# The last pairs of two squared-ReLU layers and the step to the recurrence: another order of the products, sums and transpositions

## The chip, the cores and the metric

The kernel runs on one core of a Trainium2 chip. The time is what the device needs for one execution, in microseconds (us); before the change it is 1073.29 us, the median of three runs (1073.25 to 1073.98). The engines of the core are TensorE (PE, matmuls, with its weight loads listed as PEld), VectorE (DVE), ScalarE (ACT), GpSimd (POOL) and SyncE (SP, which here only issues loads and stores). Each works through its own list of instructions in order and waits for the others through semaphores.

## The reference

A trunk of two layers over 512 tokens of width 1024, float32 throughout:

```
h = x
for layer in (0, 1):
    hn = rmsnorm(h, norm_mix[layer])
    mix = chunked_band_attention(hn, ...) if layer == 0 else rglru_block(hn, ...)
    h = h + mix
    h = h + sq_relu_mlp(rmsnorm(h, norm_mlp[layer]), w1, w2)
return rmsnorm(h, norm_final)

sq_relu_mlp(h, w1, w2):  z = relu(h @ w1);  return (z * z) @ w2      # 1024 -> 4096 -> 1024
```

The recurrent block of layer 1 projects to 2 x 1024 columns, sends one half through a causal convolution, gates and a scan, the other through a gelu, multiplies them and projects back. The change touches the two MLPs and the passage from the MLP of layer 0 to the recurrence.

## The kernel before

**Numbers.** A float32 operand is split into a high part (a rounding copy on ScalarE) and a low part (a subtraction on VectorE), and each product is three matmuls: high x high, high x low, low x high (`mm3`, line 214). So every weight passes through one ScalarE instruction (line 140, tile `wh`) and one VectorE instruction (line 143, tile `wl`).

**Weights.** They stand in one list, `plan`, in the order of use. `want(n)` (line 152) takes the next n entries and first issues the split of those ahead of them, `state["ahead"]` entries far (5 in an MLP, and in the recurrence after it). The tiles `wh` and `wl` come from a ring of five, and in an MLP from two more; a split has to wait until the matmuls on an older entry of its ring place are through. Plain entries are loaded by SP into three raw tiles (`wr`) and split there.

**The MLP** (`mlp`, line 601). The hidden width is worked through in four pairs p of two blocks of 512. An up tile `up(p, j)` (line 632) is 24 matmuls, then relu and square on ScalarE into the tile `a`. Tiles 0 to 3 of a pair make the first block, 4 to 7 the second. The down product of the pair is a 2 x 2 block product done with seven block products in place of eight: of the activation blocks 11, 12, 22 and the combinations s1 to s4, and of the weight blocks 11, 21, 22 and the combinations t1 to t4. Combinations of weights are made in place on the raw blocks (line 138), those of activations on VectorE (lines 679, 680, 682), and each activation operand is split again (`split`, line 658: tiles `h`, `h0`, `h1`, `h2` and `l`, `nn`, `g`, `f`, `c`).

`round_(p)` (line 649) does one pair: the tiles `up(p, 4)` to `up(p, 7)`, and after every second one the combinations of the chunk that is ready; then seven products through `step(name, bank, ...)`, in the order 11, 12, s1, s4, s2, s3, 22, each 24 matmuls into PSUM banks X, Z or Y. After each, `read` (line 627) adds the banks to the running result `d` in token order. A bank that goes on accumulating (X and Y) may only be written again when it has been read. In pairs 0 to 2 the up tiles 0 to 3 of the next pair are put between the later products; in the last pair there are none left, and there each product is done for one tile of 128 tokens after the other (`ts=(t,)`), with a read after each.

After the last pair of layer 0, `turns` (line 741) brings the result back to the transposed residual (`back`, 32 transpositions on TensorE, adds at line 755), and already does the norm's splits (`n1.split`), the first half of four projections of the recurrence (`open_x`, line 827: banks `xb0` to `xb3`, over tiles 4 to 7) and the squares for the norm (`n1.square`). After the last pair of layer 1, `ends` (line 776) does the final norm and the stores.

**The recurrence** (line 919 on) finishes the projections `xb0` to `xb3` with 12 matmuls each. After number 2 comes `n1.sums` (line 266: eight small matmuls that sum the squares per token, a root, a reciprocal), after number 3 `n1.rstd` (line 275: eight matmuls that spread it into a row, and a copy); then the convolutions start, whose first instruction (`xp`, line 866) reads a bank `xb` and multiplies it with the row. Later projections reuse those banks.

**The order.** The program is written as one sequence, but a scheduler works out each engine's list from it: what stands earlier goes first, and where it isn't ready by the scheduler's own reckoning, something later that is ready takes the place. Buffers are given out at the first write.

Of the kernel before, what the change touches and what calls it, by code (L numbers as in the profile page):

```python
# [18 lines left out]
KT = D // P  # L19
# [21 lines left out]
def trunk(ctx: ExitStack, tc: tile.TileContext, xT, cols, gfin, win, wqkv, wo, rwin, rga, rgx, rwo, w1, w2, out):  # L41
# [55 lines left out]
    plan = []  # L97
# [81 lines left out]
    def add_mlp(layer):  # L179
        starts.append(len(plan))  # L180
        def up_(p, j):
            c0 = 2 * p * T + j * P
            plan.append(("plain", KT, [w1[layer][:, c0 : c0 + P]]))

        for j in range(4):
            up_(0, j)
        for p in range(4):
            for j in range(4, 8):
                up_(p, j)
            srcs = [  # L190
                w2[layer][(2 * p + k) * T : (2 * p + k + 1) * T, c * T : (c + 1) * T]
                for k, c in ((0, 0), (1, 0), (0, 1), (1, 1))
            ]
            for n, kind in enumerate(("11", "21", "t1", "22", "t2", "t3", "t4")):
                for half in range(2):
                    plan.append((kind, half, srcs))
                if p < 3 and 2 <= n <= 5:
                    up_(p + 1, n - 2)
# [87 lines left out]
    with ExitStack() as actx:  # L286
# [199 lines left out]
        for k0, nk in FIRST:  # L486
            WH, WL = want(1)
# [113 lines left out]
    def mlp(ly, norm):  # L601
        with ExitStack() as mctx:
# [46 lines left out]
            def round_(p):  # L649
                A, low, raw = {}, {}, {}  # L650

                def room(n, kind, tag):
                    return (wk if tag == "nn" else zp).tile([P, 4, U], kind, name=f"{tag}{n}{ly}{p}", tag=tag)

                def place(n, h, l):
                    low[n] = (room(n, F32R, h), room(n, F32R, l))

                def split(n, ks=slice(0, 4)):
                    H, L = low[n]
                    S.copy(H[:, ks], raw[n][:, ks])  # L660
                    V.tensor_sub(L[:, ks], raw[n][:, ks], f(H[:, ks]))

                first, second = a[p, 0], None
                raw["11"], raw["s1"] = first[:, 0], first[:, 1]
                for n, tag in (("s3", "c"), ("s2", "f"), ("s4", "g")):
                    raw[n] = room(n, F32, tag)
                ins = V.tensor_sub(raw["s3"], raw["11"], raw["s1"])
                if (ly, p) == (0, 1):
                    constants(ins)
                place("11", "h0", "l")  # L670
                split("11")
                place("12", "h1", "nn")
                for j in range(4, 8):
                    up(p, j)
                    raw["12"], raw["22"] = a[p, 1][:, 0], a[p, 1][:, 1]
                    if j % 2:
                        ks = slice(j - 5, j - 3)
                        r = {n: raw[n][:, ks] for n in raw}
                        V.tensor_sub(r["s2"], r["22"], r["s3"])
                        V.tensor_sub(r["s4"], r["12"], r["s2"])  # L680
                        split("12", ks)
                        V.tensor_add(r["s1"], r["s1"], r["22"])
                Y, X = ([atp(f"{b}{ly}{p}{t}") for t in range(2)] for b in "yx")
                Z = [mmp(f"z{ly}{p}{t}") for t in range(2)]
                held = {}

                def product(name, bank, fresh, ts=(0, 1)):
                    if not held.get(name):
                        held[name] = [want(1) for part in range(2)]
                    H, L = low[name]  # L690
                    for part in range(2):
                        WH, WL = held[name][part]
                        for k in range(2):
                            for t in ts:
                                c = slice(t * P, (t + 1) * P)
                                kk_ = 2 * part + k
                                mm3(bank[t], H[:, kk_, c], L[:, kk_, c], WH(k, slice(0, T)), WL(k, slice(0, T)),
                                    fresh and kk_ == 0, kk_ == 3, True)

                def ahead(j):  # L700
                    if p < 3:
                        up(p + 1, j)


                def step(name, bank, fresh, t0, c):
                    if p < 3:
                        product(name, bank, fresh)
                    for t in range(2):
                        if p == 3:
                            product(name, bank, fresh, ts=(t,))  # L710
                        read(bank[t], t0 + t, c)


                step("11", X, True, 0, 0)
                place("s1", "h0", "l")
                split("s1")
                step("12", Z, True, 0, 0)
                place("s4", "h1", "nn")
                split("s4")
                step("s1", Y, True, 2, 1)  # L720
                place("s2", "h2", "g")
                split("s2")
                place("s3", "h0", "f")
                split("s3")
                ahead(0)
                step("s4", Y, False, 0, 1)
                place("22", "h1", "c")
                split("22")
                ahead(1)
                step("s2", X, False, 0, 1)  # L730
                ahead(2)
                if p == 3:

                    (ends if ly else turns)(step, product, X)
                    return
                step("s3", X, False, 2, 1)
                ahead(3)
                step("22", X, False, 2, 0)


            def turns(step, product, X):
                banks = [atp(f"back{i}") for i in range(2)]
                n = [0]

                def back(qs, h):
                    for q in qs:
                        x = banks[n[0] % 2]
                        n[0] += 1
                        for i in range(2):
                            c, cs = columns(2 * q + i)  # L750
                            for t in range(2):
                                j = 2 * i + t
                                PE.transpose(x[:, j * P : (j + 1) * P], dt[2 * h + t, c][:, cs], ident)
                        hv = hT2[q][:, :, h * U : (h + 1) * U]
                        V.tensor_add(hv, x.rearrange("p (i c) -> p i c", i=2), hv)

                step("s3", X, False, 2, 1)
                back(range(4), 0)
                product("22", X, False, ts=(0,))
                read(X[0], 2, 0)  # L760
                back((2, 3), 1)
                tc.keep_in_program_order(S.activation(spare, epsb, AF.Sqrt))
                product("22", X, False, ts=(1,))
                read(X[1], 3, 0)
                for m in range(4, KT):
                    n1.split(m)
                open_x(0)
                back((0, 1), 1)
                for m in range(4):
                    n1.split(m)  # L770
                open_x(1)
                for m in range(KT):
                    n1.square(m)


# [40 lines left out]
            for p in range(4):  # L816
# [1 line left out]
                    gfins = per.tile([P, 4, T], F32, name="gfins", tag="hx0")  # L818
                    nc.sync.dma_start(gfins[:, 0:2], gfin.rearrange("p (c n) -> p c n", c=2))
                round_(p)  # L820
            state.update(more=None)

    n1 = Norm("n1", C_MIX1)
    xbs = []
# [1 line left out]

    def open_x(u):
        WH, WL = want(1)
        accs = [mmp(f"xb{2 * u + i}") for i in range(2)]
        project(accs, PAIR, WH, WL, [(hnH[k], hnL[k]) for k in range(4, KT)], last=False)  # L830
        xbs.extend(accs)

    mlp(0, nm1)

# [2 lines left out]
    with ExitStack() as rctx:  # L837
# [83 lines left out]
        for u in range(4):  # L921
            WH, WL = want(2 if u > 1 else 1)
            for i in range(2):
                c = 2 * u + i
                if i == 1 and u < 3:
                    gate_weights(u + 1)
                acc = xbs[c] if c < 4 else (atp if c == 4 else mmp)(f"xb{c}")
                project([acc], PAIR[i : i + 1], WH, WL, xs if c > 3 else xs[:4], first=c > 3)
                if c < 2:
                    continue  # L930
                if c == 2:
                    n1.sums()
                if c == 3:
                    rr.append(n1.rstd())
                    for j in range(4):
                        cv[j] = conv(j, xbs[j])
                        if j >= 2:
                            gate(j - 2, *cv[j - 2])
                if c >= 4:
                    gate(c - 2, *cv[c - 2])  # L940
                    cv[c] = conv(c, acc)
                if c == 5:
                    decay(range(4))
# [81 lines left out]
```

## Time and profile before

| what | value |
|---|---|
| median of three runs | 1073.29 us |
| the profiled execution's own time | 1074.18 us |
| its span in the trace | 1072.4 us |
| busy: TensorE, VectorE, ScalarE | 1056.1, 799.9, 587.2 us |
| mean granted TensorE clock | 0.993 |
| TensorE's waits of more than 1 us after the start | 3.08, 1.88 and 2.83 us |
| TensorE's last matmul to the end of the span | 6.8 us |

The span is the time from the first to the last instruction of one execution that the profiler followed. A row of the trace gives the start and the duration of an instruction in us, engine, source line, operation, output and inputs by the names of the program's tiles, and in square brackets how long its engine had been idle before it and what ended that. Matmuls overlap: each shows some 0.39 us, but they start 0.23 us apart. The granted clock is the share of its full rate that TensorE got.

### The profile page before, as it was taken

The page shows a single profiled execution, that of the slowest core. Times are in us where ns is not written, and L with a number is a line of the kernel's source. Part 1 is how long each engine was busy: PE and PEld are TensorE (multiplying, and loading weights), DVE is VectorE, ACT ScalarE, POOL GpSimd, SP SyncE. Part 2 cuts the span into 40 slices and gives each one's busy share as a digit, 9 for nine tenths or more (in the row PEclk, how much of TensorE's full clock was granted, in tenths as well). Part 3 has the DMA queues.
Part 4 walks back from the last instruction along what each step waited for, and adds up shares of the span by engine and source line. Part 5 has one row for each costly group of instructions (what it writes and reads, how often), then busy time and mean ns, then how long its engine had stood idle before and what let it go on. Part 6 is the DMA issues. An engine that isn't in the chain of part 4 may idle for free.

```text
span 1072.4 us, 12842 instructions
## 1 busy us (share of the span) xinstructions
PE 1056.1 (98%) x4820; PEld 875.6 (82%) x4820; DVE 799.9 (75%) x1168; ACT 587.2 (55%) x886; POOL 9.0 (1%) x28
## 2 busy tenths in 40 slices
PE   9999999999999999999999999999999999999996
PEld 8888888888888888888877788888888888888884
DVE  6899779866595695596498799984396497487486
ACT  6667567555554554454454598555463454454454
POOL 0010000000000000000000000000000000000000
PEclk9999999999999999999999999999999999999998
DMA  8344253264044045045003313283136036025002
GB/s 276 99 138 132 65 177 99 79 208 126 20 154 141 7 132 177 1 127 187 1 1 117 99 60 98 79 270 87 37 98 200 17 92 202 20 81 174 1 1 79
DMA packets 128413, 111.51 MB, mean 104 GB/s; under 512 B 4320, under 2 KB 104672, under 8 KB 128352
## 3 DMA queue, kind: packets, MB, share of 16 engines
q1 hardware_dynamic: 127776, 109.99, 33.4%
q8 instruction: 38, 0.62, 0.2%
q10 hardware_dynamic: 576, 0.72, 0.2%
q14 instruction: 23, 0.19, 0.1%
HBM read 104.39 MB, written 2.10 MB: 99 GB/s over the span
## 4 chain that ended last, share of the span: by engine, by line
PE 92%; DVE 6%; ACT 1%; issue 1%; DMA 0%; POOL 0%; ACTq 0%; POOLq 0%
PE u L215 11%; PE u L216 11%; PE u L217 11%; PE x L215 5%; PE x L217 5%; PE x L216 5%; PE y L215 2%; PE y L216 2%; PE y L217 2%; PE x L437 2%; PE xb L215 1%; PE xb L217 1%; PE xb L216 1%; PE wo L215 1%; PE wo L216 1%; PE ro L215 1%
## 5 line engine op out<-in xcount | busy, mean ns | idle before, releaser
L140 ACT CAST wh<-b 128x1024 fp32r<-128x1024 f32 x112 | 117.6, 1051 | 184.9 <-PE u L216 137.0
L143 DVE TENSOR_TENSOR wl<-wr,wh 128x1024 fp32r<-128x1024 f32 (+1 forms) x122 | 146.6, 1205 | 89.8 <-ACT wh L140 78.1
L143 DVE TENSOR_TENSOR wl<-b,wh 128x1024 fp32r<-128x1024 f32 x112 | 136.6, 1222 | 102.4 <-ACT wh L140 102.4
L140 ACT CAST wh<-wr 128x1024 fp32r<-128x1024 f32 (+1 forms) x121 | 125.4, 1038 | 141.8 <-PE u L216 58.2
L215 PE MATMUL u<-hnH,wh 128*128 128x512 f32 x512 | 200.3, 391 | 0.0
L217 PE MATMUL u<-hnH,wl 128*128 128x512 f32 x512 | 199.6, 390 | 0.0
L216 PE MATMUL u<-hnL,wh 128*128 128x512 f32 x512 | 199.4, 390 | 0.0
L217 PEld LDWEIGHTS u<-hnH,wl 128*128 128x128 f32 x512 | 96.1, 188 | 20.3
L215 PEld LDWEIGHTS u<-hnH,wh 128*128 128x128 f32 x512 | 96.1, 188 | 19.7
L216 PEld LDWEIGHTS u<-hnL,wh 128*128 128x128 f32 x512 | 96.2, 188 | 19.6
L138 DVE TENSOR_TENSOR b<-b,b 128x1024 f32<-128x1024 f32 x64 | 76.7, 1223 | 1.3 <-DMA b<-in_w 1.3
L215 PE MATMUL x<-wh,h 128*128 128x512 f32 x128 | 50.1, 391 | 0.0
L216 PE MATMUL x<-wl,h 128*128 128x512 f32 x128 | 50.0, 390 | 0.0
L627 DVE SCALAR_TENSOR_TENSOR d<-x,rq,d 128x512 f32<-128x512 f32 x60 | 42.8, 745 | 3.5 <-PE x L217 3.5
L639 ACT ACTIVATE a<-u 128x512 f32<-128x512 f32 x64 | 37.8, 590 | 13.3 <-PE u L217 13.3
L640 ACT ACTIVATE a<-a 128x512 f32<-128x512 f32 x64 | 40.6, 635 | 1.8
L417 ACT ACTIVATE p<-p,mx 128x128 f32<-128x128 f32 (+1 forms) x64 | 35.2, 552 | 6.2 <-DVE mx L414 6.0
L215 PE MATMUL x<-wh,h0s 128*128 128x512 f32 x64 | 26.5, 414 | 5.9 <-DVE d L627 5.9
L660 ACT CAST h<-a 128x1024 fp32r<-128x1024 f32 (+1 forms) x32 | 26.8, 836 | 6.5 <-PE y L216 5.7
L410 DVE CUSTOM_DVE_ANT_0 p<-s,bias 128x128 f32<-128x128 f32 (+1 forms) x64 | 27.7, 485 | 3.2 <-PE s L407 2.9
L441 ACT CAST pH<-x 128x512 fp32r<-128x512 f32 (+1 forms) x48 | 21.7, 517 | 13.5 <-PE x L437 13.4
L215 PEld LDWEIGHTS x<-wh,h 128*128 128x128 f32 x128 | 24.0, 188 | 4.9
(342 smaller groups left out, 2301.4 us busy)
## 6 DMA issues: line engine op xcount, KB each, us to landing
wr<-in_w SPq DMA_DIRECT2D x64, 512.0 KB, 4.0
b<-in_w SPq DMA_DIRECT2D x64, 512.0 KB, 4.2
wr<-in_wqkv SPq DMA_DIRECT2D x20, 512.0 KB, 3.8
wr<-in_rwin SPq DMA_DIRECT2D x16, 512.0 KB, 3.4
wr<-in_wo SPq DMA_DIRECT2D x8, 512.0 KB, 4.1
wr<-in_rwo SPq DMA_DIRECT2D x8, 512.0 KB, 3.5
x<-in_xT SPq DMA_DIRECT2D x8, 256.0 KB, 3.9
bias<-in_win SPq DMA_DIRECT2D x4, 512.0 KB, 4.7
```

The lines of the kernel that those rows point to most:

```text
L138: V.tensor_sub(raw, raws[x, half], raws[y, half])
L140: S.copy(H[:, :n], raw[:, :n])
L143: low = V.tensor_sub(L[:, :n], raw[:, :n], f(H[:, :n]))
L215: PE.matmul(acc, WH, XH, start=start, stop=False, skip_group_check=more)
L216: PE.matmul(acc, WH, XL, start=False, stop=False, skip_group_check=more)
L217: PE.matmul(acc, WL, XH, start=False, stop=stop, skip_group_check=more)
L410: V.tensor_tensor_reduce(out=pt[:, seg[t] : seg[t] + n], in0=sc[t], in1=b[:, h % 4, T - n :], scale=1.0, scalar=-3.0e38, op0=ALU.add, op1= ...
L417: S.activation(pt[:, seg[t] : seg[t] + n], pt[:, seg[t] : seg[t] + n], AF.Exp, bias=mx[:, t : t + 1], accum_out=sm[:, t : t + 1],)
L627: V.scalar_tensor_tensor(d, acc, r, d, ALU.mult, ALU.add)
L639: S.activation(c, acc.rearrange("p (h c) -> p h c", h=2), AF.Relu)
L640: S.activation(c, c, AF.Square)
L660: S.copy(H[:, ks], raw[n][:, ks])
```

## The change

Six edits:

1. In the list of weights the two halves of "11" of the last pair stand between the up tiles 5 and 6 in place of behind 7. With them go the eight loads of that pair's blocks, which are issued with the first half of "11".
2. The up tiles 4 to 7 are now written behind the definition of `step`, and "11" is done inside their loop: behind tile 7 in pairs 0 to 2 (as before), behind tile 5 in the last pair.
3. In the last pair the activation combinations of the second half are made in two quarters, after tiles 6 and 7, in place of one half after tile 7.
4. In the last pair "12" is done for both token tiles together; the other products there stay one tile after the other.
5. The lookahead in the list of weights goes from 5 to 3 ahead of "s1" of the last pair, and is 4 in the recurrence (5 before).
6. In `turns`, the projections `xb0` and `xb1` are opened one after the other with the last transpositions between them; the squares of tiles 4 to 7 come ahead of `xb2`, those of 0 to 3 behind `xb3`. In the recurrence the sums come after projection 1 (before: 2) and the row after 2 (before: 3).

```diff
         for p in range(4):
-            for j in range(4, 8):
-                up_(p, j)
             srcs = [
...
+            for j in range(4, 8):
+                up_(p, j)
+                if j == (5 if p == 3 else 7):
+                    plan.extend(("11", half, srcs) for half in range(2))
-            for n, kind in enumerate(("11", "21", "t1", "22", "t2", "t3", "t4")):
+            for n, kind in enumerate(("21", "t1", "22", "t2", "t3", "t4"), 1):
...
                 place("12", "h1", "nn")
-                for j in range(4, 8):
-                    up(p, j)
-                    raw["12"], raw["22"] = a[p, 1][:, 0], a[p, 1][:, 1]
-                    if j % 2:
-                        ks = slice(j - 5, j - 3)
...
                 def step(name, bank, fresh, t0, c):
-                    if p < 3:
+                    apart = p == 3 and name != "12"
+                    if not apart:
                         product(name, bank, fresh)
                     for t in range(2):
-                        if p == 3:
+                        if apart:
                             product(name, bank, fresh, ts=(t,))
                         read(bank[t], t0 + t, c)
-                step("11", X, True, 0, 0)
+                chunks = {5: slice(0, 2), 7: slice(2, 4)} if p < 3 else {5: slice(0, 2), 6: slice(2, 3), 7: slice(3, 4)}
+                for j in range(4, 8):
+                    up(p, j)
+                    raw["12"], raw["22"] = a[p, 1][:, 0], a[p, 1][:, 1]
+                    if j in chunks:
+                        ks = chunks[j]
+                        r = {n: raw[n][:, ks] for n in raw}
+                        V.tensor_sub(r["s2"], r["22"], r["s3"])
+                        V.tensor_sub(r["s4"], r["12"], r["s2"])
+                        split("12", ks)
+                        V.tensor_add(r["s1"], r["s1"], r["22"])
+                    if j == (5 if p == 3 else 7):
+                        step("11", X, True, 0, 0)
...
                 split("s4")
+                if p == 3:
+                    state["ahead"] = 3
                 step("s1", Y, True, 2, 1)
...
-                open_x(0)
+                opening = open_x(0)
+                next(opening)
                 back((0, 1), 1)
                 for m in range(4):
                     n1.split(m)
-                open_x(1)
-                for m in range(KT):
+                next(opening)
+                for m in range(4, KT):
+                    n1.square(m)
+                for _ in open_x(1):
+                    pass
+                for m in range(4):
                     n1.square(m)
...
-            state.update(more=None)
+            state.update(more=None, ahead=4)
...
     def open_x(u):
         WH, WL = want(1)
-        accs = [mmp(f"xb{2 * u + i}") for i in range(2)]
-        project(accs, PAIR, WH, WL, [(hnH[k], hnL[k]) for k in range(4, KT)], last=False)
-        xbs.extend(accs)
+        for i in range(2):
+            xbs.append(mmp(f"xb{2 * u + i}"))
+            project(xbs[-1:], PAIR[i : i + 1], WH, WL, [(hnH[k], hnL[k]) for k in range(4, KT)], last=False)
+            yield
...
-                if c < 2:
-                    continue
-                if c == 2:
+                if c == 1:
                     n1.sums()
-                if c == 3:
+                if c == 2:
                     rr.append(n1.rstd())
+                if c == 3:
                     for j in range(4):
```

More of the change, by code (lines that the diff above doesn't have):

```diff
@@ L672, in round_ @@
                 place("12", "h1", "nn")
-                for j in range(4, 8):
-                    up(p, j)
-                    raw["12"], raw["22"] = a[p, 1][:, 0], a[p, 1][:, 1]
-                    if j % 2:
-                        ks = slice(j - 5, j - 3)
[L678 to L682, printed above, removed]
                 Y, X = ([atp(f"{b}{ly}{p}{t}") for t in range(2)] for b in "yx")
@@ L928, in trunk @@
                 project([acc], PAIR[i : i + 1], WH, WL, xs if c > 3 else xs[:4], first=c > 3)
-                if c < 2:
-                    continue
+                if c == 1:
+                    n1.sums()
                 if c == 2:
-                    n1.sums()
+                    rr.append(n1.rstd())
                 if c == 3:
-                    rr.append(n1.rstd())
                     for j in range(4):
```

## The prediction

> **What bounds the kernel now.** I read the page first, then the list of what TensorE waited for, then the time slices around those waits, and last the order of VectorE's work in them.
>
> ```profile
> span 1072.4 us, 12842 instructions
> ...
> PE 1056.1 (98%) x4820; PEld 875.6 (82%) x4820; DVE 799.9 (75%) x1168; ACT 587.2 (55%) x886; POOL 9.0 (1%) x28
> ```
>
> TensorE is busy for 98% of the span and the change takes no matmul away, so only its idle time and its slow time can be won.
>
> ```profile
> PE x L215 <- DVE d L627: 5.9, 2, 3.1
> PE xb L215 <- DVE xp L866: 1.9, 1, 1.9
> ...
> 565.41 0.47 PE L215 MATMUL x<-wh,h0s 128*128 128x512 f32 x1 [3.08 <-DVE d L627]
> 606.44 0.50 PE L215 MATMUL xb<-hnH,wh 128*128 128x512 f32 x1 [1.88 <-DVE xp L866]
> 1052.75 0.47 PE L215 MATMUL x<-wh,h0s 128*128 128x512 f32 x1 [2.83 <-DVE d L627]
> ```
>
> There are three gaps worth the name. Two are one place in the two MLPs: in the last pair, product "s3" (weights `h0s`) goes into the same banks X that "s2" filled, and must wait until VectorE has read "s2" out (line 627). The third is in the recurrence, where the next projection waits for a PSUM bank that the first convolution input (line 866) frees.
>
> ```profile
> core 0: us, PE busy (x) PEld busy (x) DVE busy (x) ACT busy (x) POOL busy (x), PEclk, DMA share, GB/s
> 534.00:561.40 27.40, 27.40 (x122) 22.50 (x121) 26.30 (x29) 16.06 (x17) 0.00 (x0) 1.00 0.00 1
> 565.40:579.80 14.40, 14.38 (x64) 11.88 (x65) 12.71 (x16) 5.04 (x7) 0.00 (x0) 0.88 0.53 165
> 606.40:620.00 13.60, 13.56 (x52) 11.00 (x53) 12.69 (x23) 9.14 (x13) 0.00 (x0) 0.87 0.12 40
> ...
> 1000.90:1022.80 21.90, 21.90 (x98) 18.14 (x97) 9.77 (x12) 8.58 (x12) 0.00 (x0) 1.00 0.00 1
> 1022.80:1049.90 27.10, 27.10 (x120) 21.96 (x118) 26.33 (x29) 14.44 (x17) 0.00 (x0) 1.00 0.00 0
> 1052.80:1065.60 12.80, 12.73 (x48) 9.99 (x48) 8.91 (x19) 6.99 (x19) 0.00 (x0) 0.87 0.22 83
> ```
>
> Two things stand here. Behind each gap the granted clock is 0.87 or 0.88, not 1.00: 0.12 x 14.4, 0.13 x 13.6 and 0.13 x 12.8 are each about 1.7 us more. And during the five products before the gap (1022.8 to 1049.9) VectorE is busy for 26.33 of 27.1 us, while in the four up tiles before (1000.9 to 1022.8) it is busy for 9.77 of 21.9. It isn't short of time in the round as a whole; it has its idle time too early. One product or up tile is 24 matmuls: 24 x 27.1 / 120 = 5.42 us.
>
> What the three gaps cost: (3.08 + 1.7) + (1.88 + 1.7) + (2.83 + 1.7) = 12.9 us. That is all that this change can win.
>
> **"11" between up tiles 5 and 6** (last pair, both layers). The prices of VectorE's work in the crowded stretch of layer 1, from 1020 to 1053:
>
> ```profile
> L143 DVE TENSOR_TENSOR wl<-b,wh 128x1024 fp32r<-128x1024 f32 x7 | 8.4, 1220 | 4.2 <-ACT wh L140 4.2
> L138 DVE TENSOR_TENSOR b<-b,b 128x1024 f32<-128x1024 f32 x6 | 7.2, 1220 | 0.0
> L627 DVE SCALAR_TENSOR_TENSOR d<-x,rq,d 128x512 f32<-128x512 f32 x4 | 2.9, 748 | 0.0
> ```
>
> Start to start a 128x1024 subtraction takes 1.13 us, a read-out 0.66, a 128x512 one 0.62 (from the rows of the chain below, 1026.54 to 1028.93). From 1023.51 to the end of the read-out at 1052.6 VectorE never stops: 29.1 us. What of it falls before the end of the last up tile once "11" has moved: two read-outs of X (1.3), half of the last pair of differences (four 128x512 operations become eight, of which four 128x256 stay behind: 2.5 less 1.5 is 1.0), and the weight work that TensorE's releases allow. A weight cast waits for a free buffer, that is for the matmuls seven weights back (the row at 1022.43 below); with "11" two up tiles earlier, the two weights that now wait for the last up tile and for "11" get their buffers 4 to 5 us earlier, so their low parts (2.3) and the block difference behind the first (1.1) go ahead too. The lookahead of 3 instead of 5 puts the last block difference (1.1) behind the read-out. 29.1 - 6.8 = 22.3 us remain, and start about 1 us after the last up tile, at 1028.9 in old times: they end at 1051.2, and TensorE wants the bank at 1049.9 (1052.75 - 2.83). That alone would leave 1.3 us of the gap.
>
> The other four block differences (4.5 us) decide. They need only raw blocks that are there and already split, so they can run while VectorE idles, as two already do now:
>
> ```profile
> 484.00:490.00 6.00, 3.60 (x3) 1.00 0.91 286
> 490.00:539.00 49.00, 0.00 (x0) 1.00 0.20 62
> 539.00:563.00 24.00, 6.76 (x6) 1.00 0.00 1
> ```
>
> (Slices of line 138 alone in layer 0: stretch, VectorE busy, count.) Each pair has eight such differences; only six of the last pair's stand after 539, so two of the three at 484 to 490 are its own, run 35 us before the weights made of them. In the new order VectorE has, between 1019 and 1029 in old times, 10 us less one low part, one block difference and 1.5 us of activation differences, some 6 us, for these four. Two of them are enough. I take the gap as gone in both layers: -4.8 and -4.5. If none goes early, 1.3 of it stays.
>
> **What now waits.** "11" was the cover between the last up tile and what is made of it. Before, "11" and "12" (10.8 us) lay ahead of "s1"; now "12" alone, 5.42.
>
> ```profile
> 1022.43 1.05 ACT L140 CAST wh<-b 128x1024 fp32r<-128x1024 f32 x1 [3.23 <-PE u L216]
> 1023.39 0.59 ACT L639 ACTIVATE a<-u 128x512 f32<-128x512 f32 x1
> 1024.01 0.63 ACT L640 ACTIVATE a<-a 128x512 f32<-128x512 f32 x1
> 1027.87 1.05 ACT L660 CAST h0s<-a 128x1024 fp32r<-128x1024 f32 x1
> ...
> 1024.68 0.69 DVE L679 TENSOR_TENSOR fs<-a,cs 128x512 f32<-128x512 f32 x1
> 1026.54 0.69 DVE L682 TENSOR_TENSOR a<-a,a 128x512 f32<-128x512 f32 x1
> 1028.93 0.75 DVE L627 SCALAR_TENSOR_TENSOR d<-x,rq,d 128x512 f32<-128x512 f32 x1
> 1029.60 1.22 DVE L661 TENSOR_TENSOR ls<-a,h0s 128x1024 fp32r<-128x1024 f32 x1
> ```
>
> From the end of the up tile (1022.8) to the first difference 1.9 us; four small ones some 1.5 (between 1.2 and 2.5: half the row, or the row); the cast `h0s` 1.0; the low part `ls` 1.2: 5.6 us. "s1" needs `ls` with its third matmul, 5.42 + 0.45 = 5.9 us after the up tile. So it just fits with nothing in between; each weight cast or subtraction in front costs about 1 us. Bounds: 0, and 2.0 (two in front) with 1.7 of slow clock behind it, 3.7 a layer. I take one in front, 0.9 a layer, because both engines' queues hold such work and take it when it is ready: +1.8. Behind the waiting matmul stand all of TensorE's, so it counts in full. "12" itself needs its last quarter only after 18 of its 24 matmuls (4.1 us), and that is made after 1.9 + 1.2: hidden, and that it runs over both token tiles together is what gives these 4.1 us; one by one it would be 2.0.
>
> The eight block loads of that pair now stand ahead of two weight loads in SP's queue:
>
> ```profile
> b<-in_w SPq DMA_DIRECT2D x64, 512.0 KB, 4.2
> ```
>
> These two weights are wanted some 30 us later, against 4.2 us a load: nothing. For the first three pairs the order is the same as before: nothing.
>
> **The step to the recurrence.**
>
> ```profile
> 599.84 0.95 PE L259 MATMUL n1ss<-ones,n1acc 128*128 128x2 f32 x8
> 604.60 0.59 ACT L280 COPY n1acc<-n1row 128x512 f32<-128x512 f32 x1
> ...
> 585.95 0.69 DVE L755 TENSOR_TENSOR h<-back,h 128x512 f32<-128x512 f32 x1 [3.19 <-PE back L753]
> 595.64 3.08 DVE L246 TENSOR_TENSOR n1acc<-n1acc,n1sq 128x512 f32<-128x512 f32 x4
> 604.56 1.23 DVE L143 TENSOR_TENSOR wl<-wr,wh 128x1024 fp32r<-128x1024 f32 x1 [3.26 <-PE n1row L278]
> 605.71 1.28 DVE L866 TENSOR_TENSOR xp<-xb,n1acc 128x512 f32<-128x512 f32 x2
> ```
>
> Sums and row each move ahead of one half projection (12 matmuls, 2.71 us). After the row comes that projection; the row's copy (0.59) and `xp` (0.66) need 1.3 to 1.5 us with the waits between, and the low part that now stands in front of `xp` is released only by the projection behind. So 1.2 us of slack, and the gap goes: -3.6. The sums, now wanted 2.71 us earlier, at 597.1, need the squares' last addition (598.7 now) 1.6 us earlier: four squares are put before the last transpositions' results, where VectorE idles 3.19 us, room for three additions of 0.6. It fits by little. Opening the projections one after the other halves the time in which the normalised tiles 4 to 7 are needed: between 0 and 1.2 us (two tiles late by a read-out); +0.3, as one is made every 0.66 us (a VectorE pass of 128x512) and used every 0.68 (three matmuls). The recurrence keeps one weight less ahead: from 0 to 1.2, +0.2, since TensorE shows no wait there.
>
> **The sum.** -12.9 + 1.8 + 0.3 + 0.2 = -10.6. The profiled execution took 1074.18 us (span 1072.4 and 1.8 around it), so 1063.6; the median of the three runs, 1073.29, lies 0.9 below it, so **1062.7**.
>
> **The rivals.**
> - *The four differences do not run early.* The order on VectorE is the scheduler's, and its stretch stays full. Then 1.3 us of each gap stays, without the slow clock or with it: 1062.7 + 2 x (1.3 to 3.0) = 1065.3 to 1068.7, say 1067. For it: 26.33 of 27.1 busy; against: the two that ran 35 us early. 0.17.
> - *The row isn't earlier in effect.* If the additions end at 598.7 as now, TensorE waits 1.6 us at the sums: 1062.7 + 3.6 = 1066.3. For it: ACT's and VectorE's other work (weights, gate weights) stands among the squares; against: the 3.19 us idle. 0.11.
> - *The slow clock after the two shorter gaps has another cause* and stays: 1062.7 + 2 x 1.7 = 1066.1. Against it: 0.87 stands right behind each of them, and 1.00 ahead. 0.03. [...]
> - *The wait moves to the head of "s1" and is longer there: slower.* What runs early may stand in front of the short chain: if six block differences come between the last up tile and `ls`, 6 x 1.13 - 0.3 = 6.5 us of wait and 1.7 of slow clock in each layer, 16.4 against 12.9 won: 1073.3 + 3.5 = 1077. It decides from 4.7 us of wait a layer on, four to five pieces in front. Against it: the chain comes first in the program, and differences are ready earlier. 0.08.
> - *Nothing changes.* If the scheduler already takes what is ready, the new program order may come out as the old one: 1073.3. Against it: the up tiles and "11" run in written order now. 0.08.
>
> **How the numbers follow.** The forecast has 0.53; its own range is 1060.4 (no new wait) to 1065.5 ("s1" waits for its upper bound, 3.7 for 0.9, in one layer). With the first three rivals it covers 1060 to 1068, 0.84. A difference of 0.2% (2.1 us) is what a measurement of this kernel can tell. Faster: 0.53 + 0.17 + 0.11 + 0.03 = 0.84; same 0.08; slower 0.08.
>
> **What would show it.** Right: no idle time before "s3" and before the projection after the row, a clock of 1.00 behind both, block differences between the third and fourth up tile, and a wait of under 2 us at the first matmuls of "s1" on `ls`. Wrong: a wait on line 627 as before, VectorE full from the last up tile to "s3", a clock below 1.00 behind "s1", or a wait at the square sums.

## The result, and the profile after

The changed kernel takes 1063.24 us (median of four runs, 1062.83 to 1063.51), beside 1073.27 for the kernel before on the same chip: a ratio of 0.9908, 95% interval 0.989 to 0.9925. That is 10.0 us less; the interval of the ratio makes it 8.0 to 11.8, so it is clear of the noise. The profiled execution took 1062.83 us, 11.35 less than the profiled one of before.

The page of the profile after, its span and busy times, and then the list of what TensorE waited for (waiting engine and line, what released it; total, times, longest):

```profile
span 1060.8 us, 12851 instructions
...
PE 1051.4 (99%) x4820; PEld 870.4 (82%) x4820; DVE 799.1 (75%) x1176; ACT 587.4 (55%) x888; POOL 9.7 (1%) x28
```

```profile
PE warm L472 <- POOL ones L85: 1.0, 1, 1.0
PE s L408 <- DVE v L354: 0.4, 1, 0.4
PE ga L217 <- ACT xcH L890: 0.3, 1, 0.3
PE ga L218 <- DVE xcL L891: 0.3, 1, 0.3
PE s L408 <- DMA kl<-kl: 0.3, 1, 0.3
```

All three gaps are gone. What is left is 1.0 us at the start, 0.4 and 0.3 in the attention, and two waits of 0.3 us at the gates of the recurrence; the first and one of 0.3 in the attention were there before. (Lines from 190 on have moved by two, in the recurrence by some 15.) Behind the three places the clock is whole, as the slices of the changed kernel show (stretch, length, TensorE busy, granted clock):

```profile
561.40:575.00 13.60, 13.48 (x72) 1.00 0.65 194
598.50:612.00 13.50, 13.49 (x59) 1.00 0.11 39
1043.00:1054.00 11.00, 11.00 (x50) 1.00 0.25 97
```

Where the time came from can be read by the start of the same matmul in both profiled executions, in us from the start of the span:

| matmul | before | after | lead |
|---|---|---|---|
| square sums ahead of the MLP of layer 0 | 266.48 | 266.62 | -0.14 |
| first matmul of "s3", last pair, layer 0 | 565.41 | 561.51 | 3.90 |
| first of projection `xb0` | 579.82 | 575.47 | 4.35 |
| last of the projections `xb` | 636.75 | 629.32 | 7.43 |
| first of the output projection `ro` | 685.29 | 678.51 | 6.78 |
| first of "s3", last pair, layer 1 | 1052.75 | 1043.09 | 9.66 |
| last matmul of all | 1065.14 | 1053.75 | 11.39 |

At "s3" of layer 0 the lead holds the gap (3.08) and 0.9 us of eight transpositions that stood ahead of it and now come behind; the slow clock's share is gained between there and `xb0`.

How the gap before "s3" closed stands in VectorE's work of the last pair of layer 1, changed kernel:

```profile
1011.97 1.22 DVE L143 TENSOR_TENSOR wl<-b,wh 128x1024 fp32r<-128x1024 f32 x1
1013.22 3.62 DVE L138 TENSOR_TENSOR b<-b,b 128x1024 f32<-128x1024 f32 x3
1016.76 1.22 DVE L143 TENSOR_TENSOR wl<-b,wh 128x1024 fp32r<-128x1024 f32 x1
...
1019.25 3.61 DVE L138 TENSOR_TENSOR b<-b,b 128x1024 f32<-128x1024 f32 x3
...
1041.42 0.74 DVE L629 SCALAR_TENSOR_TENSOR d<-x,rq,d 128x512 f32<-128x512 f32 x1
1042.96 0.16 DVE L807 TENSOR_TENSOR fs<-fs 128x1 f32<-128x1 f32 x1 [0.79 <-ACT fsq L797]
```

All six block differences run in two threes: the first from the third up tile (tile 6, from 1010.24) into the fourth, the second from the fourth to just behind its end (1021.12). Before, they stood between 1027.8 and 1050.7 among the read-outs. What lets them run is the split of weight "22": t2 is made in place on that block, and t3 and t4 read it. The low parts of its two halves start at 1011.97 and 1016.76, which is 9.2 and 4.4 us ahead of the end of the last up tile. In the kernel before they started at 1023.51 and 1030.73, 1.1 and 8.3 us behind that end (1022.46). The read-out that "s3" waits for starts at 1041.42; TensorE needs it at 1043.09. VectorE even idles behind it.

The head of "s1", where I had expected a new wait, on TensorE of the changed kernel:

```profile
1026.33 0.39 PE L219 MATMUL z<-wh,nn 128*128 128x512 f32 x1
1026.56 0.39 PE L217 MATMUL x<-wh,h2s 128*128 128x512 f32 x1
1026.79 0.39 PE L218 MATMUL x<-wl,h2s 128*128 128x512 f32 x1
1027.04 0.50 PE L217 MATMUL y<-wh,h0s 128*128 128x512 f32 x1
...
1028.08 0.39 PE L217 MATMUL x<-wh,h2s 128*128 128x512 f32 x1
1028.30 0.40 PE L218 MATMUL x<-wl,h2s 128*128 128x512 f32 x1
1028.54 0.40 PE L219 MATMUL y<-wh,ls 128*128 128x512 f32 x1
```

`ls` is late (it is made from 1027.05 to 1028.27, 1.3 us after the place of the third matmul of "s1", 1027.0), but nothing waits: the scheduler put the matmuls ahead that need only the high part `h0s`, and four of product "s2".

And the row of the changed kernel, on TensorE, ScalarE and VectorE:

```profile
596.42 1.05 PE L280 MATMUL n1row<-ident,rt 128*128 128x128 f32 x8
597.51 0.59 ACT L282 COPY n1acc<-n1row 128x512 f32<-128x512 f32 x1 [3.51 <-PE n1row L280]
598.13 1.29 DVE L881 TENSOR_TENSOR xp<-xb,n1acc 128x512 f32<-128x512 f32 x2 [3.02 <-ACT n1acc L282]
```

The matmuls of projection 3 start from 597.23 to 599.84; the first `xp` is done by 598.8.

### The profile page after: what moved, and what is told of

Read it like the earlier page. It is cut to its first block, busy times and chain, and to the rows that moved or that the text cites. A ratio compares the mean times of both kernels' runs of the same rounds, so it can differ in the third digit from the quotient of the medians.

```text
span 1060.8 us, 12851 instructions
## 1 busy us (share of the span) xinstructions
PE 1051.4 (99%) x4820; PEld 870.4 (82%) x4820; DVE 799.1 (75%) x1176; ACT 587.4 (55%) x888; POOL 9.7 (1%) x28
## 4 chain that ended last, share of the span: by engine, by line
PE 91%; DVE 4%; DMA 2%; ACT 2%; issue 1%; ACTq 0%; SPq 0%; DVEq 0%
PE u L217 11%; PE u L219 11%; PE u L218 11%; PE x L218 5%; PE x L217 5%; PE x L219 5%; PE y L217 3%; PE y L218 3%; PE y L219 3%; PE x L439 2%; PE wo L217 1%; PE wo L218 1%; PE ro L217 1%; PE xb L217 1%; PE ro L219 1%; PE xb L219 1%
## 5 line engine op out<-in xcount | busy, mean ns | idle before, releaser
L662 ACT CAST h<-a 128x1024 fp32r<-128x1024 f32 (+2 forms) x34 | 27.2, 799 | 6.7 <-PE y L218 5.8
L218 PEld LDWEIGHTS x<-wl,h 128*128 128x128 f32 x128 | 24.0, 188 | 4.9
```

Of the source, the lines that this page charges most:

```text
L218: PE.matmul(acc, WH, XL, start=False, stop=False, skip_group_check=more)
```

## The experiments

Each kernel was timed in three rounds against the kernel before on the same chip, but for the last. The kernels stand in three groups, each on one chip. The kernel before had a median of 1074.14 us beside the first four below; of 1071.32 beside the held kernel, those with the old row and the old opening, and the one with "12" done apart; and of 1071.76 beside the rest. Why that differs so much is told in the last section. The kernels without gaps agree within 1 us, so I compare these with each other.

**One part alone.** First only the last pairs:

```diff
-                if p == 3:
-                    state["ahead"] = 3
-            state.update(more=None, ahead=4)
+            state.update(more=None)
   (and edit 6, the step to the recurrence, undone)
```

> Only the edits on the last pairs ("11" between up tiles 5 and 6, quarters, "12" over both token tiles); lookahead 5 and the old step to the recurrence. My theory, each gap has its own edit: the two gaps before "s3" are gone with their slow clock (9.3 us), the gap of 1.9 us before the projection behind the row stays: between 1064.0 (1073.3 - 9.3) and 1066.8 (1063.2 + 3.6). Rival, it is the shorter lookahead that closes the gaps: 2 to 3 us of wait on line 627's read-out stay in each layer, about 1070.

Measured 1064.26 us, ratio 0.9916 (0.9899 to 0.9934), and one wait left:

```profile
PE xb L217 <- DVE xp L873: 1.9, 1, 1.9
```

So the last pairs' edits close both gaps before "s3" by themselves, and the third gap is the step's own.

Then only the step to the recurrence, edits 1 to 5 undone:

```diff
-                    if j == (5 if p == 3 else 7):
+                    if j == 7:
                         step("11", X, True, 0, 0)
...
-                    apart = p == 3 and name != "12"
+                    apart = p == 3
...
-                if p == 3:
-                    state["ahead"] = 3
```

> Only the step to the recurrence (opening one by one, squares in two parts, sums and row each one projection earlier). My theory: one gap of 1.9 us and its slow clock go, both gaps before "s3" stay at about 3 us: 1069.7 (1073.3 - 3.6), at most 1072.5 (1063.2 + 9.3). Rival, the row's move gains only while the last pair is also early: 1073.

Measured 1071.41 us beside 1074.14, ratio 0.9979 (0.9969 to 0.9988): 2.7 us, between the 1.9 of the gap alone and the 3.6 with its slow clock. The two other gaps are as before.

```profile
PE x L215 <- DVE d L627: 5.9, 2, 3.1
```

Then only the lookahead, edits 1 to 4 and 6 undone, which is the kernel before with

```diff
+                if p == 3:
+                    state["ahead"] = 3
                 step("s1", Y, True, 2, 1)
...
-            state.update(more=None)
+            state.update(more=None, ahead=4)
```

> Only the lookahead (3 from "s1" of the last pair on, 4 in the recurrence). My theory: 1.1 to 2.3 us of weight work goes behind the read-out of "s2", so the gaps before "s3" shrink from about 3 to 1 or 2 us: 1071 with the slow clock still behind them, 1067.7 without. Rival, the lookahead is what closes the gaps: no wait on line 627, 1064.

Measured 1066.08 us, ratio 0.9932 (0.9915 to 0.9948): between the rival's 1064 and my 1067.7. The waits are nearer to the rival's none than to my 1 to 2 us each:

```profile
PE xb L215 <- DVE xp L873: 1.9, 1, 1.9
...
PE x L215 <- DVE d L627: 0.9, 2, 0.7
```

The two gaps shrink from 5.9 to 0.9 us together, and no slow clock shows behind what is left: the profiled run's mean granted clock is 0.999, as that of the changed kernel. In VectorE's list of layer 1 there are six low parts of weights and five block differences between the last up tile and the read-out, before seven and six: 2 x 1.13 = 2.3 us less, where the prediction had counted 1.1. 2.83 - 2.27 = 0.6, measured 0.7. Some of that work comes back at the end: from TensorE's last matmul to the end of the span it is 7.8 us here, against 7.1 in the changed kernel.

**Without the lookahead.** Is it needed, then?

```diff
-                if p == 3:
-                    state["ahead"] = 3
-            state.update(more=None, ahead=4)
+            state.update(more=None)
```

> The changed kernel with the lookahead at 5 throughout. My theory: nothing waits, since the block differences run early anyhow: 1063.2 to 1064. Rival, the lookahead is needed: waits on line 627 come back, 1066 to 1070.

Measured 1062.97 us (1062.62 to 1063.03), ratio 0.9902 (0.9883 to 0.9922), no wait over 0.4 us but the start's. Not needed: the early "11" and the short lookahead are two cures for one gap.

**What makes the early "11" work.** The block differences for t2, t3 and t4 of the last pair are kept behind the last activation difference on VectorE, by an order between the two instructions:

```diff
-                V.tensor_sub(raw, raws[x, half], raws[y, half])
+                dif = V.tensor_sub(raw, raws[x, half], raws[y, half])
+                if kind != "t1" and state["hold"] is not None:
+                    after(dif, state["hold"])
...
-                        V.tensor_add(r["s1"], r["s1"], r["22"])
+                        done = V.tensor_add(r["s1"], r["s1"], r["22"])
+                        state["hold"] = done if (p, j) == (3, 7) else None
```

> The changed kernel, but the block differences for t2, t3 and t4 of the last pair are held on VectorE until the last quarter of the activation differences is made, as the first rival of the prediction has it. My theory, their early place is what empties the crowded stretch: six differences of 1.13 us more after the last up tile, VectorE full until the read-out of "s2", 2 to 3 us of wait before "s3" in each layer, with the slow clock 1068 to 1071. Rival, the earlier "11" alone is enough: 1063.2.

Measured 1065.71 us (1065.61 to 1065.89), ratio 0.994 (0.9922 to 0.9957): 2.2 to 2.4 us more than two kernels of the same group with nothing held (1063.56 and 1063.29, below), but less than I expected. A wait before "s3" is back in layer 1 alone (line 631 is the read-out here):

```profile
PE x L219 <- DVE d L631: 0.7, 1, 0.7
```

That is 0.7 of the 2.2 to 2.4 us. In the step to the recurrence new waits of 0.5 and 0.3 us stand, and behind TensorE's last matmul the kernel takes 8.0 us to the end, against 7.1 with nothing held. The lookahead was still at work. With both taken away (this edit, and lookahead 5):

> The changed kernel with both taken away: the block differences of the last pair held until the last activation differences, and lookahead 5. "11" stays early. My theory: "11" alone cures through what may run early, and with the lookahead's 2.3 us back in the stretch the wait before "s3" is 0.7 + 2.3 = 3.0 us again in a layer, with slow clock: 1069 to 1072. Rival, the earlier "11" itself moves enough: 1065 to 1066.

Measured 1074.9 us (1074.69 to 1075.43) beside 1071.76, ratio 1.0027 (1.0014 to 1.0039): the whole gain is gone, and more, although "11" stands early and the step to the recurrence is the new one. All ten runs had a granted clock of 0.993 or 0.994, which the kernel before had in some of its runs only. The waits, and VectorE in layer 1:

```profile
PE x L219 <- DVE d L631: 7.3, 2, 3.8
```

```profile
1023.24 1.22 DVE L145 TENSOR_TENSOR wl<-b,wh 128x1024 fp32r<-128x1024 f32 x1 [3.55 <-ACT wh L142]
...
1029.12 0.42 DVE L715 TENSOR_TENSOR fs<-a,cs 128x256 f32<-128x256 f32 x1 [3.29 <-ACT a L644]
...
1051.47 1.22 DVE L138 TENSOR_TENSOR b<-b,b 128x1024 f32<-128x1024 f32 x1
1052.60 1.40 DVE L631 SCALAR_TENSOR_TENSOR d<-x,rq,d 128x512 f32<-128x512 f32 x2
```

VectorE idles 3.55 and 3.29 us ahead of the last differences, and then the six block differences stand in the crowded stretch once more; the last of them ends just ahead of the read-out. So with the six held the early "11" gains nothing. It gains because it lets weight work run in VectorE's idle time. Whether that work comes early through buffers freed earlier or through the earlier place of "11" in the list was not tested apart.

**The step to the recurrence, part by part.** Sums and row back behind projections 2 and 3:

```diff
-                if c == 1:
+                if c < 2:
+                    continue
+                if c == 2:
                     n1.sums()
-                if c == 2:
-                    rr.append(n1.rstd())
                 if c == 3:
+                    rr.append(n1.rstd())
```

> The changed kernel with sums and row back in their old place (after projections 2 and 3), the squares in the new order. My theory: the row's copy and the first convolution input stand bare again, 1.4 to 1.9 us of wait and 1.7 of slow clock where it comes: 1064.6 to 1066.8. Rival, the earlier squares or the lookahead had closed that gap: 1063.2.

Measured 1064.22 us, ratio 0.9926 (0.9909 to 0.9944): the wait of 1.9 us is back, and a low part of a weight stands in front of `xp` again:

```profile
600.74 1.23 DVE L143 TENSOR_TENSOR wl<-wr,wh 128x1024 fp32r<-128x1024 f32 x1 [3.26 <-PE n1row L280]
601.88 1.28 DVE L881 TENSOR_TENSOR xp<-xb,n1acc 128x512 f32<-128x512 f32 x2
```

Against the two kernels of this group that have the row early (1063.56 and 1063.29, below) it costs 0.7 to 0.9 us, not 1.9: the two waits of 0.3 us at the gates, which the changed kernel has, aren't in this kernel's list; that the convolution gets ahead during the gap would explain it, but was not tested. No slow clock came behind the gap: the granted clock was 1.00 from 598.42 to 608.66.

The old opening and the squares all behind it, with the new place of sums and row:

```diff
-                opening = open_x(0)
-                next(opening)
+                open_x(0)
                 back((0, 1), 1)
...
-                next(opening)
-                for m in range(4, KT):
-                    n1.square(m)
-                for _ in open_x(1):
-                    pass
-                for m in range(4):
+                open_x(1)
+                for m in range(KT):
                     n1.square(m)
   (and `open_x` as in the kernel before)
```

> The changed kernel with the old opening of the projections and the squares after all of it, sums and row in the new place. My theory: the squares' last addition comes too late for the earlier sums, up to 1.6 us of wait before them (or TensorE takes projection work forward): 1063.5 to 1066.5. Rival, the squares were early enough anyhow: 1063.2.

Measured 1063.56 us, ratio 0.992 (0.9902 to 0.9938), no new wait: 0.3 us beside the changed kernel's 1063.24, too little to tell. With the last pairs early, the squares come in time in either order. Not so where "11" is late: the kernel before with nothing but the lookahead and the new place of sums and row (both shown above, as the changed kernel has them),

> The kernel before with the lookahead of 3 and 4 and the earlier sums and row alone: "11" in its old place, old opening, old squares. If the lookahead and the early "11" are two cures for the same gap, this comes within 2 us of the changed kernel: waits of under 1 us before "s3" as with the lookahead alone, the gap of 1.9 us before the convolution gone: 1064.0 to 1065.0. If the early "11" is needed once the row is early: 1066 or more.

measured 1065.86 us, ratio 0.9944 (0.9926 to 0.9962), 0.9 above the most that two cures for one gap would give. The row's gap is gone, and smaller waits have come in its place:

```profile
PE x L215 <- DVE d L627: 0.9, 2, 0.7
PE n1ss L259 <- DVE n1acc L246: 0.7, 1, 0.7
PE xb L215 <- ACT hnH L235: 0.4, 1, 0.4
```

**The small edits.** "12" of the last pair one token tile after the other:

```diff
-                    apart = p == 3 and name != "12"
+                    apart = p == 3
```

> The changed kernel with "12" of the last pair done one token tile after the other. My theory: its last quarter is wanted 2.0 us after the last up tile in place of 4.1 and made after about 2.7 to 3.1: 0.7 to 1.1 us of wait in each layer, 1064.6 to 1065.4. Rival, the scheduler fills the wait with other matmuls, as it did before "s1": 1063.2.

Measured 1063.29 us, ratio 0.9918 (0.9897 to 0.9939): nothing that can be told. And the differences of the second half in one piece:

```diff
-                chunks = {5: slice(0, 2), 7: slice(2, 4)} if p < 3 else {5: slice(0, 2), 6: slice(2, 3), 7: slice(3, 4)}
+                chunks = {5: slice(0, 2), 7: slice(2, 4)}
```

> The changed kernel with the activation differences of the second half made in one half after tile 7, as in the other pairs. My theory: "12" wants its second half 2.7 us after the last up tile, and it is made after 3.1: 0.4 to 0.8 us of wait a layer, 1064.0 to 1064.8. Rival, the scheduler fills it with other matmuls: 1063.2.

Measured 1063.76 us (1062.21 to 1064.37), ratio 0.9917 (0.9895 to 0.9938): nothing that can be told either. The traces show a little: from its first matmul to the next product's, "12" takes 5.8 us in both kernels and both layers, against 5.4 in layer 1 of the changed kernel, and matmuls of "12" on the high part `h` are put ahead of those on `nn`. So 0.3 to 0.4 us a layer is lost, less than I expected, since the scheduler has other matmuls to put in.

**The kernel before, profiled once more.** With one gap of 1.9 us the first and the third of these kernels, and the one with the old row, showed no slow clock behind it (1.00 at it and behind it), while the kernel before had. Its slow stretches behind the three gaps all last 3.41 us, at a granted clock of 0.50. They begin at 565.92, 606.88 and 1054.03, which is 12 and 131 times 3.413 us apart, as if on a grid. In the 3.41 us ahead of each TensorE was busy for 0.51, 1.54 and 1.28 us; the first and the third, from the first profile (stretch, length, TensorE busy, granted clock):

```profile
562.51:565.92 3.41, 0.51 (x2) 1.00 0.04 12
565.92:569.33 3.41, 3.41 (x9) 0.50 0.42 143
...
1050.62:1054.03 3.41, 1.28 (x6) 1.00 0.02 5
1054.03:1057.44 3.41, 3.41 (x10) 0.50 0.00 0
```

> The kernel before once more, unchanged, for a second profile of it. My theory: the gaps are the same (3.1, 1.9 and 2.8 us), but whether the clock is slow behind each depends on where it lies on a fixed grid of 3.41 us: slow when over half of one grid window is idle. So the gap of 1.9 us is slowed in about half of all executions. Rival, the gap's length alone decides: all three slowed again.

It took 1073.06 us (a single execution). The gaps are the same, 3.1, 1.9 and 2.8 us, but the clock is slow behind the second and third only. The slices of the grid (stretch, length, TensorE busy, granted clock), around the first gap and the second:

```profile
560.94:564.36 3.42, 1.80 (x13) 1.00 0.00 0
564.36:567.77 3.41, 1.97 (x9) 1.00 0.47 145
567.77:571.18 3.41, 3.41 (x17) 1.00 0.44 134
...
601.90:605.32 3.42, 1.54 (x12) 1.00 0.00 0
605.32:608.73 3.41, 3.41 (x8) 0.50 0.48 154
608.73:612.14 3.41, 3.41 (x16) 1.00 0.00 0
```

The longer gap falls into two slices, busy for 1.80 and 1.97 us each: no slow clock. The shorter one lies in one slice, busy for 1.54: the next slice is at half clock. The first profile of the kernel before has the same 1.54, and the kernel with the last pairs' edits alone has its gap across a border:

```profile
603.47:606.89 3.42, 1.54 (x11) 1.00 0.00 1
606.89:610.30 3.41, 3.41 (x10) 0.50 0.46 153
```

```profile
597.46:600.87 3.41, 3.12 (x18) 1.00 0.37 129
600.87:604.28 3.41, 1.82 (x8) 1.00 0.36 113
604.28:607.70 3.42, 3.42 (x17) 1.00 0.12 41
```

The rival, that the length alone decides, has fallen. That the gap of 1.9 us is slowed in about half of all executions is open: it was in two of the five profiles that have it, too few to tell.

The slices at the end of two programs, behind the last matmul, give two more readings (the lookahead alone, then the changed kernel with lookahead 5):

```profile
1055.87:1059.28 3.41, 1.54 (x7) 1.00 0.39 150
1059.28:1062.69 3.41, 0.00 (x0) 1.00 0.63 241
...
1052.85:1056.26 3.41, 1.28 (x6) 1.00 0.33 128
1056.26:1059.68 3.42, 0.00 (x0) 0.50 0.47 179
```

Here a slice busy for 1.54 us was followed by a whole clock, one of 1.28 by half. So 1.54 stands on both sides; the ends of matmuls are modelled, and these runs don't show where the border is, nor that it is the half that I expected.

## Why the prediction was right, and where it wasn't

1062.7 was forecast for the median, 1063.24 measured, well within the likeliest case's own range.

- **The three gaps, -12.9.** Place and cause were right, and all three are gone. From the leads in the table: 4.35 and 0.14 at `xb0` for the first (4.8 forecast), 3.1 more up to the end of the projections for the third (3.6), 4.6 from `ro` to the last matmul with "s3" of layer 1 between (4.5).
- **The four differences that run early** decided, as said: without them and with the lookahead at 5 the gaps are 3.5 and 3.8 us (the held kernel). The account of them was not exact. They do not need only blocks that are there, but the split of "22", which in the kernel before came only behind the last up tile and now comes ahead of its end. And in the changed kernel all six run early, none behind the read-out, where the prediction had put one. My stretch without them and with the short lookahead left 1.3 us a layer; measured 0.7 in one layer and no wait that the list shows in the other.
- **The lookahead's 1.1 us** was mis-sized: it is 2.3, one low part more, and alone it takes 5.0 of the 5.9 us. I had counted it as a small part of what the early "11" gains; it is a second cure, and the first makes it superfluous.
- **The head of "s1", +1.8,** was wrong. The chain is late, by 1.3 us a layer where 0.9 was forecast: the first difference comes 2.8 us after the up tile (1021.12 to 1023.91), not 1.9, as a low part stands ahead of it. But I had held the order of TensorE's matmuls fixed. The scheduler put six matmuls in, and nothing waits.
- **"12" over both token tiles** was said to give 4.1 us of cover that it needs. It hardly needs it: done apart, "12" takes 0.3 us more a layer, not 0.7 to 1.1.
- **The recurrence, +0.2 and +0.3.** Some 1.2 us were lost there in all: 0.5 up to the end of the projections (3.6 less 3.1) and 0.65 between `xb` and `ro`, where the two waits at the gates stand. Neither forecast term shows by itself: with the lookahead at 5 the time is 1062.97, with the old opening 1063.56. The wait behind the row seems to have been no pure loss, as VectorE and ScalarE could get ahead in it; this is argued from the gates' waits, not tested.
- **The slow clock, 1.7 a gap,** was right for the profiled execution and is not right for the median, as it comes behind a gap in some executions only. The rival that it has another cause than the gap's length had 0.03; that was too little, though the place in time counts with the length: in the second profile of the kernel before, no slow clock stands behind 3.1 us of gap, and half clock behind 1.9. That the profiled execution had all three slow stretches, and probably lay 0.9 above the median for it, I did not ask about.

That the median came within 0.5 us is partly luck, as the misses cancel. For the profiled execution the forecast was 0.8 too high (1063.6 against 1062.83): 1.8 too much for "s1", 0.7 too little for the recurrence and 0.3 for the first gap. And I had put the median 0.9 below the profiled execution; it came 0.4 above it, 1.3 the other way. The median of the kernel before itself moved from 1071.32 to 1074.14 between the groups.

## What to carry to other kernels

When an engine is full just ahead of a wait, look for the idle time in front of the full stretch and for work that could be made ready there; moving a product of another engine can be the way to let it run, and two edits that do this are not two gains. When costing a wait on an engine whose order a scheduler fills, ask which of its instructions are ready, before taking the wait as idle time. And a gap's price can have a part that depends on its place in time (here 1.7 us or nothing behind gaps of 1.9 and 3.1 us): compare medians of several executions, not two profiles.

## What the runs showed of the hardware

In the two profiles of the kernel before, five of the six gaps have a slice of 3.41 us behind them in which TensorE's granted clock was 0.50, and ahead of it one with a clock of 1.00. In the one ahead TensorE had been busy for 0.51, 1.54 and 1.28 us (first profile) and for 1.54 and 0.96 us (second). At the sixth gap, the first of the second profile, the slices were busy for 1.80 and 1.97 us and the clock stayed at 1.00. So it did at the gap of 1.9 us in three other kernels, where the least busy slice had 1.82 us (the last pairs alone), 1.79 (the lookahead alone) and 2.33 (the old row). At the end of a program 1.54 was followed by 1.00; closer than this the runs don't tell the two cases apart.

The slices don't keep a fixed place in the program: in two executions of the kernel before the first gap ends at 565.41 and 565.80 us, and slices begin at 562.51 and 564.36. A gap of 1.9 us was followed by half clock in the two profiles of the kernel before, worth 1.7 us more (3.41 x 0.50), and not in the three other kernels; the one of 3.1 us was in one of the two profiles, and not in the other.

The runs' own granted clocks fit. The kernel before ran from 1069.44 to 1074.95 us over the groups: 1069.4 to 1070.4 at a clock of 0.999, 1070.4 to 1072.0 at 0.997, 1072.9 to 1073.9 at 0.995 or 0.996, and 1073.1 to 1075.0 at 0.993 or 0.994. By my estimate these are steps of about one slow slice, 1.7 us, and three such slices are worth 5.1 of the 5.5. The held kernel with lookahead 5, whose gaps of 3.5 and 3.8 us are longer than a slice, was at 0.993 or 0.994 in all ten runs; the kernel before was at 0.993 in the profile with three slow slices. The changed kernel, without gaps, stays within 0.7. The clock isn't all, though: the kernel with the differences in one half, also without these gaps, ran from 1062.21 to 1064.37 at 0.998 or 0.999, and nothing here explains that.
